# The hybrid decoder step: first tile's rows squared ahead of the second tile's, sampled rows' last scaling placed behind the copy of the compact scores

## Chip, cores, metric

One of the eight cores of a Trainium2 chip runs the whole program. The metric is the device time of one launch in microseconds (us).

## What is computed

One trunk layer for a prompt of 2048 tokens and for 64 sampled tokens (8 sequences of 8), all in float32:

```python
h = rms_norm(x, g_mix_pre)
proj = einsum('btd,de->bte', h, w_in)       # split: q, k, v | gq, gk, gv, gr, low-rank gate
attn = sliding window attention with sinks (8 heads of 64, 2 kv heads, window 128)
o, s_new = gla_chunked(gq, gk, gv, log_a, s0)          # 4 heads, dk 64, dv 128
gla_out = rms_norm(o, g_gla) * silu(gr)
mix = einsum('bte,ed->btd', concat([attn, gla_out]), w_out)
x = x + rms_norm(mix, g_mix_post)
h = rms_norm(x, g_ffn_pre)
u = relu(einsum('btd,df->btf', h, w_up))
f = einsum('btf,fd->btd', u * u, w_down)
x = x + rms_norm(f, g_ffn_post)
```

The outputs are the prompt's and the samples' rows, their last 128 keys and values, and the states of the gated linear attention (GLA).

## The kernel before

Rows lie in 17 tiles: 16 of 128 prompt rows (numbers 0 to 15) and one of the 64 sampled rows (number 16, `NB`). Each float32 product is made of three (high by high, high by low, low by high part), so an operand is first split: ScalarE (ACT) copies the high part, VectorE (DVE) subtracts it for the low part. TensorE (PE) is busy nearly all the time; the other engines prepare its operands and take its sums out of PSUM.

The program has these stages, one after the other: projection and attention (`unit`, `sample_unit`); GLA with the rest of the projection woven in (`gla`, `sampled`, `products`); the output projection with the residual rows (`out_projecting`, `residual`); the up projection (`up`, with `opening` as its first block); the down projection (`down`).

The code is written as generators that are advanced by `next` and `run`. Within what they write, a scheduler of the framework sets the order on each engine. `tc.issue_after(x)` ties an instruction behind another in that order and adds no semaphore between them. Each engine runs its instructions in order, so one that waits holds all behind it. DMAs are issued by SyncE (SP), also in order.

**GLA, one tile.** `gla` makes score products into the banks `gl` and `gh`, six masked copies on VectorE (`put_level`, COPY_PREDICATED) gather them into the compact scores `AH`, and VectorE (`put[0]`, line 1173) and ScalarE (lines 1172 and 1174) copy these into `AT`. Two VectorE instructions (line 1179) then bring the state `S` up to date. The products `o` read `AT`. `finish_out` ends a tile: squares, their mean to the power -0.5 on GpSimd (POOL; `rsqrt_mean`), and four scalings `og` on VectorE (line 1088), one for each head, whose transposes (`ogT`) follow. For the sampled rows the same function runs with `i == NB`: it reads the bank `s_ob`, writes the scaled rows into `gp_s`, and its transposes are put off by `S_WAIT[0]` further steps. It runs beside the GLA of a prompt tile.

**Output projection.** The tiles are taken in the order `B_ORDER` = 0, 4, 1, 5, 2, 6, 3, 7, 16, 8, 12, ... . A tile has 48 products (two halves of 512 columns, 8 parts of the sum, three each), into the banks `a` or `b` in turn. The first two tiles are multiplied at the end of the GLA stage. `mixed` then takes a tile's two banks: two squares (ScalarE, line 1412), their sum and the power -0.5, two scalings `x<-out` (VectorE, line 1419), and the add of the input row `bx` (line 1420). `residual` goes on: a square of the new row (`bjunk`, line 1510), the power, the scaling by `gpre` (line 1513), which gives the row that PE transposes (`xnT`, line 1523), and copies of the transposed row (`ht`, `H`).

The first tile (0) has its new rows early: `mixed_first` runs in the GLA stage and its result goes by a DMA (`mt<-x_first`, line 1422) into a place in the `mt` buffer of the third tile. What is left of it in the loop is the square of that place, the scaling and the transposes. The second tile (4) has all of `residual` left; it waits for its input rows (`bx<-in_x_prompt`). The `mt` buffers alternate, so the load of the fifth tile's operand (`mt<-mix_d`) waits until the third tile's products and the scaling that reads the first tile's rows are through.

Of the kernel before, what the change touches and what calls it, by code (L numbers as in the profile page):

```python
# [16 lines left out]
ALU = mybir.AluOpType  # L17
# [4 lines left out]
P = 128  # L22
# [3 lines left out]
NB = T // P  # L26
# [89 lines left out]
def f32(ap):  # L116
    return ap.bitcast(F32)
# [23 lines left out]
def hybrid_step_kernel(ctx: ExitStack, tc: tile.TileContext, I, O):  # L141
    nc = tc.nc
# [11 lines left out]
    def rows(i):  # L154
        return min(P, NTOK - i * P)
# [12 lines left out]
    def bank(shape, kind, name):  # L168

        return ps.tile(shape, F32, tag=kind, name=name, bufs=1 if kind in "de" else 2)  # L170
# [3 lines left out]
    def next_bank(kinds, name):  # L174
        turns[kinds] += 1
        return bank([P, 512], kinds[(turns[kinds] - 1) % len(kinds)], name)
# [26 lines left out]
    def rsqrt_mean(pool, out, ssq, n, m, c=1, vector=nc.vector):  # L203

        v = pool.tile([P, c], F32, tag="rs_v", name="rs_v", bufs=4)
        vector.tensor_scalar(v[:n], ssq, 1.0 / m, EPS, op0=ALU.mult, op1=ALU.add)  # L206
        e = half[:n] if c == 1 else half[:n].to_broadcast([n, c])
        nc.gpsimd.tensor_tensor(out, v[:n], e, op=ALU.pow)  # L208

    def folded(out, p_, scalar=nc.scalar, vector=nc.vector):  # L210

        scalar.activation(out, p_[NS:], AF.Copy)
        vector.tensor_tensor(out, out, p_[:NS], op=ALU.add)  # L213
        return out
# [68 lines left out]
    def load_x(i):  # L283
        xs_in[i] = x = sp.tile([P, D], F32, tag="x", name=f"x_{i}", bufs=2)
        nc.sync.dma_start(x[: rows(i)], x_rows(i))
        ropes[i] = sp.tile([P, 2, HD], F32, tag="rope", name=f"rope_{i}", bufs=4)
        nc.sync.dma_start(ropes[i], I["c_rope"][i])
# [386 lines left out]
    def run(products, n=None):  # L674
        deque(products if n is None else islice(products, n), 0)
# [95 lines left out]
    early, late = (deque((c, k) for c in cs for k in range(KT)) for cs in (G_EARLY, G_LATE))  # L771
# [303 lines left out]
    def finish_out(i, og_src, sg, n, kind):  # L1075

        ssq = sp.tile([P, 4], F32, tag="ossq", name=f"ossq_{i}", bufs=2)
        junk = sp.tile([P, P], mybir.dt.bfloat16, tag="ojunk", name=f"ojunk_{i}", bufs=1)
        for h in range(4):
            nc.scalar.activation(junk[:n], og_src(h), AF.Square, accum_out=ssq[:n, h : h + 1])  # L1080
        rs = sp.tile([P, 4], F32, tag="ors", name=f"ors_{i}", bufs=2)
        rsqrt_mean(sp, rs[:n], ssq[:n], n, P, 4)
        if i == NB:
            yield 44, True
            yield 44, True
        og = next(ogs) if i < NB else gp_s[:, :512].rearrange("p (h d) -> p h d", h=4)
        for h in range(4):
            nc.vector.scalar_tensor_tensor(
                og[:n, h, :], og_src(h), rs[:n, h : h + 1], sg[:n, h * P : (h + 1) * P],
                op0=ALU.mult, op1=ALU.mult,  # L1090
            )
        for _ in range(S_WAIT[0] if i == NB else 1):
            yield 44, True
        pt = bank([P, 4, P], kind, f"ogT_{i}")
        for h in range(4):
            te.transpose(pt[:, h, :n], og[:n, h, :], ident[:n, :n])
        if i == NB - 1:
            hi, lo = late_mix
            nc.vector.tensor_copy(hi, pt)
            nc.vector.tensor_tensor(lo, pt, f32(hi), op=ALU.subtract)  # L1100
        else:
            mo = next(mos)
            nc.scalar.activation(mo[:, :, :n], pt[:, :, :n], AF.Copy)
            nc.sync.dma_start(mix_d[i][:, 4:8, :], mo[:, :, :n])
# [303 lines left out]
    def mixed(i, banks, x, x1, junk, ssq, gpost, pool, scalar=nc.scalar, vector=nc.vector):  # L1408
        n = rows(i)
        for c in range(2):  # L1410
            cc = slice(c * 512, (c + 1) * 512)
            scalar.activation(junk[:n, cc], banks[c][:n], AF.Square, accum_out=ssq[:n, c : c + 1])
        vector.tensor_tensor(ssq[:n, 0:1], ssq[:n, 0:1], ssq[:n, 1:2], op=ALU.add)
        rs = ssq[:n, 3:4]
        rsqrt_mean(pool, rs, ssq[:n, 0:1], n, D, vector=vector)
        yield
        for c in range(2):
            cc = slice(c * 512, (c + 1) * 512)
            vector.scalar_tensor_tensor(x1[:n, cc], banks[c][:n], rs, gpost[c][:n], op0=ALU.mult, op1=ALU.mult)
        vector.tensor_tensor(x[:n], x1[:n], x[:n], op=ALU.add)  # L1420
        if x1_first and i == B_ORDER[0]:
            placing[:] = [nc.sync.dma_start(x1_first[0], x)]
        nc.sync.dma_start(x1_d[i], x[:n])

    wo, pre, ogs_of, mixes, late_mix, g_mix, put, placing, x1_first = {}, {}, {}, {}, [], [], [], [], []
    wo_parts = iter(())
    early = []
# [46 lines left out]
    def ht_place(name):  # L1474
        return keep.tile([P, 7, KT // 2, P], F32, tag="st", name=name, bufs=1)
# [21 lines left out]
    def residual(i, banks, tensor=nc.tensor, scalar=nc.scalar, vector=nc.vector):  # L1497

        n = rows(i)
        x = res_x.pop(i, None) or load_x(i)[0]  # L1500
        ssq = sp.tile([P, 48], F32, tag="ssq", name=f"bssq_{i}", bufs=2)
        junk = sp.tile([P, D], mybir.dt.bfloat16, tag="junk", name=f"bjunk_{i}", bufs=1)
        x1 = R["x"].tile([P, D], F32, tag="x1", name=f"x1_{i}", bufs=2)
        if i == NB:
            banks = [folded(x1[:NS, c * 512 : (c + 1) * 512], p_) for c, p_ in enumerate(banks)]
        if banks:
            g = g_mix if tensor is nc.tensor else [gpost[:, c * 512 : (c + 1) * 512] for c in range(2)]
            yield from mixed(i, banks, x, x1, junk, ssq, g, sp, scalar, vector)
        rs = ssq[:, 3:5]
        scalar.activation(junk[:n], x[:n], AF.Square, accum_out=ssq[:n, 2:3])  # L1510
        yield
        rsqrt_mean(sp, rs[:n, 1:2], ssq[:n, 2:3], n, D, vector=vector)
        vector.scalar_tensor_tensor(x1[:n], x[:n], rs[:n, 1:2], gpre[:n], op0=ALU.mult, op1=ALU.mult)
        yield
        sb, j, second = i // 8, i % 4, i % 8 >= 4
        q = slice(j * P, (j + 1) * P)
        if i < NB and not second and i:
            sums[sb, j] = ht_place(f"ht_{i}")
        for h in range(2):
            kk = slice(h * 4, h * 4 + 4)  # L1520
            pt = (bank([P, 512], "ce"[h], f"xnT_{i}_{h}") if te is tensor else next_bank("cdce", f"xnT_{i}_{h}")).rearrange("p (k t) -> p k t", k=4)
            for k in range(4):
                tensor.transpose(pt[:, k, :n], x1[:n, (h * 4 + k) * P : (h * 4 + k + 1) * P], ident[:n, :n])
            if i == NB:
                split_copy(xsT[:, kk, :NS], xsT[:, kk, NS:], pt[:, :, :NS], vector)
                continue
            ht = sums[sb, j]
            scalar.activation(ht[:, (6, 2)[h] if second else h], pt, AF.Copy)
            if sb == 0 and not second:
                split_copy(H[h + 1][0][:, :, q], H[h + 1][1][:, :, q], pt, vector)  # L1530
        if i == NB or not second:
            return
        yield
        for out, a, b in ((4, 6, 0), (6, 2, 6), (5, 2, 4), (3, 1, 5)):
            vector.tensor_tensor(ht[:, out], ht[:, a], ht[:, b], op=ALU.subtract)
        kept = slice(2 * (sb == 0), 7)
        nc.sync.dma_start(h_d[sb][:, kept, :, q], ht[:, kept])
# [55 lines left out]
    for n, i in enumerate(B_ORDER[2:]):  # L1593
        early.append((i, []))
        mixing = out_projecting(nc.tensor, i, early[-1][1])
        run(mixing, 24 if i == B_ORDER[-1] else 48)
        if n == 0:
            second = residual(*early.pop(1))
            next(second)
            next(second)  # L1600
        elif n == 1:
            run(second)
        if n != 1:
            run(residual(*early.pop(0)))
        run(mixing)
        if n == len(B_ORDER) - 5:
            with tc.issue_after(loaded.ins):
                first_up = load_up(0, 0)
            with tc.issue_after(first_up.ins):
                gpost = gains(I["g_mix_post"][0], 0, "gpost")  # L1610
            split_up(0, 0, 0)
            split_up(0, 0, 1)
            fetch_h(0, 5)
# [575 lines left out]
```

## Time and profile before

| | |
|---|---|
| time, median of 3 runs | 2207.52 us (2206.16 to 2207.61) |
| time of the profiled execution | 2206.11 us |
| its span | 2204.0 us |
| granted TensorE clock | 0.996 |
| busy: PE, DVE, ACT, POOL | 98%, 69%, 55%, 12% |

The span is what the instructions cover; 2.11 us of the execution's time lie outside it. In a timeline a row has a start, the time that a run of equal instructions covers, the engine, the line and the tiles (out<-in); in brackets stands how long the engine was idle before it and what released it.

### The profile page before, as it was taken

The page shows a single profiled execution, that of the slowest core. Times are in us where ns is not written, and L with a number is a line of the kernel's source. Part 1 is how long each engine was busy: PE and PEld are TensorE (multiplying, and loading weights), DVE is VectorE, ACT ScalarE, POOL GpSimd, SP SyncE. Part 2 cuts the span into 40 slices and gives each one's busy share as a digit, 9 for nine tenths or more (in the row PEclk, how much of TensorE's full clock was granted, in tenths as well). Part 3 has the DMA queues.
Part 4 walks back from the last instruction along what each step waited for, and adds up shares of the span by engine and source line. Part 5 has one row for each costly group of instructions (what it writes and reads, how often), then busy time and mean ns, then how long its engine had stood idle before and what let it go on. Part 6 is the DMA issues. An engine that isn't in the chain of part 4 may idle for free.

```text
span 2204.0 us, 34115 instructions
## 1 busy us (share of the span) xinstructions
PE 2163.2 (98%) x11784; PEld 1864.7 (85%) x11784; DVE 1531.4 (69%) x3101; ACT 1219.1 (55%) x2626; POOL 263.0 (12%) x418
## 2 busy tenths in 40 slices
PE   8999999999999999899999999999999999999998
PEld 7999989999998888688888887887888888888886
DVE  5888868777775665788888655547676666555566
ACT  5889867566664444555555544435444554444444
POOL 2566512121111100000000000000000000000000
PEclk9999999999999999999999999999999999999999
DMA  6344232214336665768777677758554334766685
GB/s 228 131 137 156 96 106 70 68 64 148 136 125 237 223 208 190 239 228 277 260 261 270 232 236 225 240 182 260 180 195 149 138 144 148 238 201 193 194 269 185
DMA packets 240185, 411.53 MB, mean 187 GB/s; under 512 B 25924, under 2 KB 142124, under 8 KB 235900
## 3 DMA queue, kind: packets, MB, share of 16 engines
q1 hardware_dynamic: 240012, 409.35, 55.9%
q8 instruction: 93, 1.52, 0.3%
q14 instruction: 80, 0.66, 0.1%
HBM read 265.82 MB, written 143.99 MB: 186 GB/s over the span
## 4 chain that ended last, share of the span: by engine, by line
PE 85%; DVE 6%; ACT 4%; DMA 2%; issue 1%; POOL 1%; SPq 0%; DVEq 0%; ACTq 0%; POOLq 0%
PE dn L130 26%; PE gproj L130 10%; PE uc L130 7%; PE ua L130 7%; PE out L1318 6%; PE proj L130 5%; PE ue L130 4%; PE ud L130 4%; PE ub L130 4%; PE av L130 1%; PE sam L130 1%; PE dsam L130 1%; PE o L130 1%; PE pT L130 1%; PE sc L130 1%
## 5 line engine op out<-in xcount | busy, mean ns | idle before, releaser
L130 PE MATMUL dn<-o0t,o0s 128*128 128x512 f32 x896 | 349.3, 390 | 2.8 <-DVE f L1891 1.5
L130 PE MATMUL dn<-o1t,o0s 128*128 128x512 f32 x896 | 349.5, 390 | 0.3 <-DVE o1t L219 0.2
L130 PE MATMUL dn<-o0t,o1s 128*128 128x512 f32 x896 | 349.4, 390 | 0.0
L219 DVE TENSOR_TENSOR o1s<-rs,o0s 128x512 fp32r<-128x512 f32 x224 | 154.7, 691 | 227.8 <-ACT o0s L218 223.7
L218 ACT ACTIVATE o0s<-rs 128x512 fp32r<-128x512 f32 x224 | 141.1, 631 | 305.5 <-PE dn L130 282.3
L130 PE MATMUL gproj<-wg,gxh 128*128 128x384 f32 x1024 | 272.5, 342 | 0.3 <-DVE gp_s L213 0.3
L130 ACT ACTIVATE st<-st 128x512 f32<-128x512 f32 x224 | 141.2, 630 | 140.7 <-DVE st L130 136.6
L130 PEld LDWEIGHTS dn<-o0t,o0s 128*128 128x128 f32 x896 | 168.3, 188 | 40.6 <-DVE f L1891 2.4
L130 PEld LDWEIGHTS dn<-o1t,o0s 128*128 128x128 f32 x896 | 168.2, 188 | 37.0 <-DVE o1t L219 1.1
L130 PEld LDWEIGHTS dn<-o0t,o1s 128*128 128x128 f32 x896 | 168.2, 188 | 35.0
L130 PEld LDWEIGHTS gproj<-wg,gxh 128*128 128x128 f32 x1024 | 183.8, 188 | 4.1 <-issue 3.1
L130 PE MATMUL uc<-H,s 128*128 128x512 f32 x768 | 186.8, 391 | 0.4 <-DVE s L130 0.4
L130 PE MATMUL gproj<-wg,gxl 128*128 128x384 f32 x576 | 186.0, 340 | 0.2 <-DVE gp_s L213 0.2
L130 PE MATMUL ua<-H,w 128*128 128x512 f32 x744 | 179.2, 390 | 0.0
L130 PEld LDWEIGHTS uc<-H,s 128*128 128x128 f32 x768 | 142.9, 188 | 31.2 <-DVE s L130 0.8
L130 PEld LDWEIGHTS ua<-H,w 128*128 128x128 f32 x744 | 139.7, 188 | 29.5
L1318 PE MATMUL out<-wo,mt 128*128 128x512 f32 x680 | 158.6, 392 | 0.0
L219 DVE TENSOR_TENSOR o1t<-rt,o0t 128x512 fp32r<-128x512 f32 x224 | 153.5, 685 | 7.0 <-ACT o0t L218 6.9
L208 POOL TENSOR_TENSOR frs<-rs_v,half 128x1 f32<-128x1 f32 (+1 forms) x13 | 10.1, 787 | 1214.4 <-DVE rs_v L206 694.5
L1318 PEld LDWEIGHTS out<-wo,mt 128*128 128x128 f32 x680 | 126.5, 188 | 26.1
L218 ACT ACTIVATE o0t<-rt 128x512 fp32r<-128x512 f32 x224 | 138.3, 618 | 8.9 <-DMA rt<-t_d 7.2
L130 DVE TENSOR_TENSOR st<-st 128x512 f32<-128x512 f32 x160 | 110.6, 692 | 27.0 <-ACT st L130 22.6
(405 smaller groups left out, 4322.3 us busy)
## 6 DMA issues: line engine op xcount, KB each, us to landing
s_d<-st SPq DMA_DIRECT2D x32, 1792.0 KB, 8.7
rs<-s_d SPq DMA_DIRECT2D x224, 256.0 KB, 2.8
raw<-in_w_up SPq DMA_DIRECT2D x64, 512.0 KB, 4.3
rt<-t_d SPq DMA_DIRECT2D x128, 256.0 KB, 4.1
rt<-in_w_down SPq DMA_DIRECT2D x96, 256.0 KB, 3.1
t<-in_w_down SPq DMA_DIRECT2D x64, 256.0 KB, 4.0
t_d<-t SPq DMA_DIRECT2D x32, 512.0 KB, 3.2
hraw<-h_d SPq DMA_DIRECT2D x20, 512.0 KB, 5.1
```

The lines of the kernel that those rows point to most:

```text
L130: ins = call(*a, **k)
L208: nc.gpsimd.tensor_tensor(out, v[:n], e, op=ALU.pow)
L218: nc.scalar.activation(hi, src, AF.Copy)
L219: vector.tensor_tensor(lo, src, f32(hi), op=ALU.subtract)
L1318: te.matmul(banks[c], x, w[:, c * 512 : (c + 1) * 512], start=k + u == 0, stop=k == KT - 1 and u == len(products) - 1,)
```

## The change

Two edits. In `finish_out`, the four scalings of the sampled rows are tied behind `put[0]`, the VectorE copy of the compact scores of the prompt tile that runs beside them. In the loop of the output projection, the first tile's generator is advanced to its square before the second tile's is begun, and run to its end after the second tile's square.

```diff
@@ finish_out
         for h in range(4):
-            nc.vector.scalar_tensor_tensor(
-                og[:n, h, :], og_src(h), rs[:n, h : h + 1], sg[:n, h * P : (h + 1) * P],
-                op0=ALU.mult, op1=ALU.mult,
-            )
+            with tc.issue_after(put[0].ins) if i == NB else nullcontext():
+                nc.vector.scalar_tensor_tensor(
+                    og[:n, h, :], og_src(h), rs[:n, h : h + 1], sg[:n, h * P : (h + 1) * P],
+                    op0=ALU.mult, op1=ALU.mult,
+                )
@@ the loop over B_ORDER[2:]
         if n == 0:
-            second = residual(*early.pop(1))
+            first_rows = residual(*early.pop(0))
+            next(first_rows)
+            second = residual(*early.pop(0))
             next(second)
             next(second)
+            run(first_rows)
         elif n == 1:
             run(second)
-        if n != 1:
+        else:
             run(residual(*early.pop(0)))
```

What this does to the order on the engines, at three places. First VectorE in the GLA stage, where the sampled rows end (`gp_s` their scaled rows, `AH` the compact scores, `AT` and `S` as above). Before:

```order
L206 TENSOR_SCALAR rs_v<-ossq_6665 64x4
L1088 SCALAR_TENSOR_TENSOR gp_s<-s_ob,ors_6671,s_sg 64x128
L1063 COPY_PREDICATED AH<-c_1573,gl_6679 128x128
L1088 SCALAR_TENSOR_TENSOR gp_s<-s_ob,ors_6671,s_sg 64x128
L1063 COPY_PREDICATED AH<-c_1573,gl_6679 128x64x2
L1088 SCALAR_TENSOR_TENSOR gp_s<-s_ob,ors_6671,s_sg 64x128
L1063 COPY_PREDICATED AH<-c_1573,gl_6679 128x32x4
L1088 SCALAR_TENSOR_TENSOR gp_s<-s_ob,ors_6671,s_sg 64x128
L1063 COPY_PREDICATED AH<-c_1573,gl_6679 128x16x8
L1063 COPY_PREDICATED AH<-c_1573,gh_6680 128x8x16
L1063 COPY_PREDICATED AH<-c_1573,gh_6680 128x4x32
L1173 COPY AT<-AH 64x4x64
```

The same place after the change:

```order
L206 TENSOR_SCALAR rs_v<-ossq_6665 64x4
L1063 COPY_PREDICATED AH<-c_1573,gl_6679 128x128
L1063 COPY_PREDICATED AH<-c_1573,gl_6679 128x64x2
L1063 COPY_PREDICATED AH<-c_1573,gl_6679 128x32x4
L1063 COPY_PREDICATED AH<-c_1573,gl_6679 128x16x8
L1063 COPY_PREDICATED AH<-c_1573,gh_6680 128x8x16
L1063 COPY_PREDICATED AH<-c_1573,gh_6680 128x4x32
L1174 COPY AT<-AH 64x4x64
L1180 SCALAR_TENSOR_TENSOR S_4967<-S_4968,dec_4983,ds_6707 128x128 x2
L1089 SCALAR_TENSOR_TENSOR gp_s<-s_ob,ors_6671,s_sg 64x128 x4
L1073 COPY_PREDICATED AH<-dmsk,dg_6831 128x256
```

The four scalings leave their places between the copies and stand behind the update of the state.

Second, ScalarE at the start of the loop (`out_0_9241` and `out_1_9465` are the second tile's banks, `bx_9554` its rows, `mt_9446` holds the first tile's rows, `xnT_0_9628` its transposed rows, `out_0_9556` is a bank of the third tile, `raw_0_0` a block of `w_up`). Before:

```order
L218 ACTIVATE mt_9548<-mt_9548 128x1024
L1412 ACTIVATE bjunk_9607,bssq_9606<-out_0_9241 128x512
L1412 ACTIVATE bjunk_9607,bssq_9606<-out_1_9465 128x512
L1510 ACTIVATE bjunk_9607,bssq_9606<-bx_9554 128x1024
L1510 ACTIVATE bjunk_9621,bssq_9620<-mt_9446 128x1024
L1580 ACTIVATE w_0_0_10699<-raw_0_0_10693 128x1024
L1412 ACTIVATE bjunk_9772,bssq_9771<-out_0_9556 128x512
L1412 ACTIVATE bjunk_9772,bssq_9771<-out_1_9581 128x512
L1528 ACTIVATE ht_9547<-xnT_0_9628 128x512
```

After:

```order
L218 ACTIVATE mt_9548<-mt_9548 128x1024
L1511 ACTIVATE bjunk_9607,bssq_9606<-mt_9446 128x1024
L1413 ACTIVATE bjunk_9611,bssq_9610<-out_0_9241 128x512
L1413 ACTIVATE bjunk_9611,bssq_9610<-out_1_9465 128x512
L1529 ACTIVATE ht_9547<-xnT_0_9628 128x512
L1511 ACTIVATE bjunk_9611,bssq_9610<-bx_9554 128x1024
L218 ACTIVATE H_0_9515<-xnT_0_9628 128x4x128
L1529 ACTIVATE ht_9547<-xnT_1_9636 128x512
L218 ACTIVATE H_0_9517<-xnT_1_9636 128x4x128
L1413 ACTIVATE bjunk_9772,bssq_9771<-out_0_9556 128x512
L218 ACTIVATE mt_9715<-mt_9715 128x1024
L1413 ACTIVATE bjunk_9772,bssq_9771<-out_1_9581 128x512
```

The square of the first tile's rows goes ahead of the second tile's squares, the two high parts of `w_up` fall behind the third tile's squares, and the split of the fifth tile's operand (`mt_9715`) now stands between those squares. On VectorE the scaling of the first tile's rows (line 1513, now 1514) goes ahead of the add of the second tile's input rows. On SP the second block of `w_up` and the fifth tile's operand go ahead of the store of the second tile's rows (`x_d<-bx`).

Third, TensorE in the fourth tile's products (`out_0_9644`), at the first tile's transposes. Before, they stand behind 17 of the fourth tile's products:

```order
L1318 MATMUL out_0_9644<-wo_2_9177,mt_9548 128x512 x2
L1318 MATMUL out_0_9644<-wo_2_9178,mt_9548 128x512
L1523 MATMUL xnT_0_9628<-ident,x_0_9622 128x128 x4
L1523 MATMUL xnT_1_9636<-ident,x_0_9622 128x128 x4
L1318 MATMUL out_0_9644<-wo_2_9177,mt_9548 128x512
```

After, behind the first four:

```order
L1319 MATMUL out_0_9644<-wo_1_9058,mt_9548 128x512
L1319 MATMUL out_0_9644<-wo_1_9059,mt_9548 128x512
L1319 MATMUL out_0_9644<-wo_1_9058,mt_9548 128x512 x2
L1524 MATMUL xnT_0_9628<-ident,x_0_9608 128x128 x4
L1524 MATMUL xnT_1_9636<-ident,x_0_9608 128x128 x4
```

The transposes stand 13 products earlier.

## The prediction

> **What bounds the kernel now.** I read the page first, then what TensorE waits for, then the timeline of each engine around its waits. The page:
>
> ```profile
> span 2204.0 us, 34115 instructions
> PE 2163.2 (98%) x11784; PEld 1864.7 (85%) x11784; DVE 1531.4 (69%) x3101; ACT 1219.1 (55%) x2626; POOL 263.0 (12%) x418
> ```
>
> TensorE is busy for 2163.2 of 2204.0 us, and the change takes no product away. It can only gain from the 40.8 us in which TensorE stands, and only where TensorE itself waits. Three rows of the waits of TensorE (what waits, for whom, us in total, times, longest):
>
> ```profile
> PE ua L130 <- ACT s L130: 3.0, 1, 3.0
> PE xnT L1523 <- DVE x L1513: 1.6, 1, 1.6
> PE o L130 <- DVE S L1179: 1.4, 2, 0.7
> ```
>
> The second and one of the two waits of the third belong to the places that the change touches. The first comes later, in the opening of the up projection, and matters for whether a gain is kept.
>
> **The first tile's rows.** The timeline of TensorE at the start of the loop:
>
> ```profile
> 709.50 15.02 PE L1318 MATMUL out<-wo,mt 128*128 128x512 f32 x65
> 726.10 1.06 PE L1523 MATMUL xnT<-ident,x 128*128 128x128 f32 x8 [1.58 <-DVE x L1513]
> 726.92 7.34 PE L1318 MATMUL out<-wo,mt 128*128 128x512 f32 x31
> 734.89 7.32 PE L1318 MATMUL out<-wo,mt 128*128 128x512 f32 x31
> ```
>
> 65 products (48 of the third tile, 17 of the fourth) end at 724.52, and the transposes wait 1.58 us for the scaled rows. A product takes 15.02 / 65 = 0.231 us. Why the rows are late is seen on ScalarE and VectorE:
>
> ```profile
> 712.76 1.06 ACT L218 ACTIVATE mt<-mt 128x1024 fp32r<-128x1024 f32 x1 [7.17 <-DMA mt<-mix_d]
> 713.72 0.58 ACT L1412 ACTIVATE bjunk<-out 128x512 bf16<-128x512 f32 x1
> 721.50 1.06 ACT L1510 ACTIVATE bjunk<-bx 128x1024 bf16<-128x1024 f32 x1 [6.53 <-DVE bx L1420]
> 722.68 1.06 ACT L1510 ACTIVATE bjunk<-mt 128x1024 bf16<-128x1024 f32 x1
> ```
> ```profile
> 715.00 0.16 DVE L1413 TENSOR_TENSOR bssq<-bssq 128x1 f32<-128x1 f32 x1
> 716.08 1.41 DVE L1419 SCALAR_TENSOR_TENSOR x<-out,bssq,wo 128x512 f32<-128x512 f32 x2 [0.72 <-POOL bssq L208]
> 720.17 1.23 DVE L1420 TENSOR_TENSOR bx<-x,bx 128x1024 f32<-128x1024 f32 x1 [2.69 <-DMA bx<-in_x_prompt]
> 724.67 1.28 DVE L1513 SCALAR_TENSOR_TENSOR x<-mt,bssq,gpre 128x1024 f32<-128x1024 f32 x1 [0.59 <-POOL bssq L208]
> ```
>
> The first tile's square (of `mt`, 722.68) stands behind the second tile's (of `bx`, 721.50), for which ScalarE idles 6.53 us: the second tile's add waits for its input rows, which land at 720.08 (the chain's row below). The first tile's rows need none of that.
>
> With the change the first tile's square starts at A, when the copy of `mt` is done (712.76 + 1.06 = 713.82) and its own rows have landed. From there: 1.18 to the next ScalarE instruction (722.68 - 721.50), 1.28 for the second tile's two squares (715.00 - 713.72), 1.08 to its scalings (716.08 - 715.00), 1.41 for these, 1.28 for the first tile's scaling, 0.15 to the transposes (726.10 - 725.95). Together 6.38 us. The power of the first tile runs on GpSimd meanwhile. The landing of the first tile's rows is not in a row by itself; its neighbours in SP's queue are:
>
> ```profile
> 711.27 0.50 SPq L1422 DMA_DIRECT2D mt<-x_first  x1
> 712.46 0.78 SPq L1479 DMA_DIRECT2D gpre<-in_g_ffn_pre  x1
> 715.08 0.69 SPq L1576 DMA_DIRECT2D raw<-in_w_up  x1
> 721.81 0.43 SPq L1576 DMA_DIRECT2D raw<-in_w_up  x1
> 726.10 0.33 SPq L1278 DMA_DIRECT2D mt<-mix_d  x1
> ```
> ```profile
> mt<-mix_d SPq DMA_DIRECT2D x3, 512.0 KB, 3.8
> x_d<-bx SPq DMA_DIRECT2D x3, 512.0 KB, 2.6
> x_d<-x_first SPq DMA_DIRECT2D x1, 512.0 KB, 4.2
> ```
> ```profile
> 713.28 6.80 DMA bx<-in_x_prompt
> ```
>
> Transfers of the same 512 KB take 2.6 us from issue to landing alone and 4.2 in company, so the rows issued at 711.27 land between 713.9 and 715.5; I take 714.7, midway, since the one ahead in the queue is already under way. The transposes are then ready at 714.7 + 6.38 = 721.1 (bounds 720.3 to 721.9). The gain `gpre` must be there by 719.7; it is issued between `mt<-x_first` and `bx`, and `bx` has landed by 713.28 + 6.80 = 720.08, so at the very worst the rows are 0.4 us later, 721.5. TensorE reaches the transposes 13 products earlier than before, at 724.52 - 13 x 0.231 = 721.5. So the wait of 1.58 us goes, with 0.4 us to spare by my values and up to 0.4 us of wait left at the late bound of the landing. **Term 1: -1.58 us, bounds -1.2 and -1.58.**
>
> What else moves there. The second tile's banks come free at 714.7 + 1.18 + 1.28 + 1.08 + 0.7 (half of 1.41) = 718.9 and 719.7 instead of 716.8 and 717.5; the fourth tile's first product needs the first of them at 709.50 + 48 x 0.231 = 720.6, so 1.7 us of cover remain. The second tile's add would start at 720.9 in place of 720.17, and its square stands behind the first copy of the transposed rows and so starts about 722.6, 1.1 us later than 721.50; its own transposes come only after the 31 products that end at 726.92 + 7.34 = 734.26, so this is covered by several us. The second `w_up` block is issued some 6 us earlier (right behind 715.08 instead of 721.81), behind `bx` in the queue; nothing on TensorE needs it in this stage. The fifth tile's operand is issued when the third tile's products and the first tile's scaling are through, about 721, not 726.10, and lands near 721 + 3.8 = 724.8. That matters since the third tile's second square now waits behind its split on ScalarE: 1.06 + 0.64 + 1.08 for split, square and power, two VectorE instructions of 1.23 and half a pair of scalings, 0.7, make 5.9, so the third tile's first bank is free near 730.7. The fifth tile needs it at 734.89 less what is gained, 732.6: 1.9 us of cover.
>
> **The sampled rows.** The rows of TensorE, VectorE and ScalarE there:
>
> ```profile
> 475.09 0.86 PE L130 MATMUL gh<-XQ,XK 128*64 128x64 f32 x20
> 481.01 0.49 PE L130 MATMUL o<-gp,AT 128*128 128x128 f32 x2 [0.74 <-DVE S L1179]
> 493.60 0.46 PE L130 MATMUL ogT<-ident,gp_s 64*128 64x64 f32 x4
> ```
> ```profile
> 476.04 0.16 DVE L206 TENSOR_SCALAR rs_v<-ossq 64x4 f32<-64x4 f32 x1 [1.89 <-ACT ojunk L1080]
> 477.32 0.34 DVE L1088 SCALAR_TENSOR_TENSOR gp_s<-s_ob,ors,s_sg 64x128 f32<-64x128 f32 x1 [1.12 <-POOL ors L208]
> 477.59 0.43 DVE L1063 COPY_PREDICATED AH<-c,gl 128x128 f32<-128x128 uint8 x1
> 480.36 0.61 DVE L1179 SCALAR_TENSOR_TENSOR S<-S,dec,ds 128x128 f32<-128x128 f32 x2
> 480.99 0.45 DVE L1073 COPY_PREDICATED AH<-dmsk,dg 128x256 f32<-128x256 uint8 x1
> ```
> ```profile
> 480.56 0.40 ACT L1174 ACTIVATE AT<-AH 64x256 f32<-64x256 f32 x1
> ```
>
> VectorE waits 1.12 us for GpSimd's power with the six copies of the compact scores behind it, though what the copies read was finished at 475.95. The copies start at 477.59, `AT` is whole at 480.96 on ScalarE, and TensorE waits 0.74 us for it. How long the copies take with nothing between them is seen one tile later:
>
> ```profile
> 498.50 1.59 DVE L1063 COPY_PREDICATED AH<-c,gl 128x128 f32<-128x128 uint8 x4
> 501.38 0.41 ACT L1174 ACTIVATE AT<-AH 64x256 f32<-64x256 f32 x1
> ```
>
> From the first copy to `AT` are 501.79 - 498.50 = 3.29 us there, against 480.96 - 477.59 = 3.37 here: the three scalings between them cost 0.08 in all, and what is gained is the start. With the change the copies follow `rs_v`, at about 476.25, and `AT` is whole at 479.54. TensorE wants it at 481.01 - 0.74 = 480.27, so the wait goes with 0.7 us to spare (0.6 if the copies took 3.37 as now). Behind the state (480.97 - 1.4 = 479.55) the four scalings then take about 4 x 0.3 = 1.2 us, so the next copy starts at 480.75, still ahead of 480.99; their transposes come at 493.60, 12.8 us later. **Term 2: -0.74 us, the same at both ends.**
>
> **The sum.** -1.58 - 0.74 = -2.32 us. The profiled execution took 2206.11 (2.11 outside its span), 1.41 under the median of the runs and 0.05 under the lowest. On its scale I expect 2203.8; on that of the median, 2207.52 - 2.32 = **2205.2**. That is 0.1%, under the 0.2% (4.4 us) which a measurement of this kernel can tell from no change.
>
> **Rivals.** *A, late in part.* The first tile's rows are ready after TensorE arrives and 0.2 to 1.5 us of the wait stay. For: my spare is 0.4 us on an inferred landing. Against: `mt<-x_first` has only one transfer ahead of it. Time 2205.4 to 2206.7, say 2206.0.
>
> *B, given back later.* TensorE arrives 2.32 us sooner at the opening of the up projection, where it waits for ScalarE and VectorE anyway:
>
> ```profile
> 884.83 1.03 PE L1523 MATMUL xnT<-ident,x 128*128 128x128 f32 x8
> 903.37 0.73 PE L130 MATMUL ua<-H,s 128*128 128x512 f32 x2 [2.97 <-ACT s L130]
> ```
>
> If what ends that wait does not come sooner, the gain turns into a longer wait: 2207.5. Against it: that work (the last tiles' rows, stored, fetched again and split) starts from the last sums and transposes of TensorE before 885.9, so it should move with them.
>
> *C, slower.* The transposes now stand 3.0 us earlier in TensorE's row of products, and so do all products behind them. If what the first tile's scaling needs (its rows, or `gpre`) lands late, TensorE meets the wait early. Point: with term 2 counted, the kernel is slower from a wait of 2.32, scaled rows ready after 723.8, which is a landing of `mt<-x_first` after 717.4 or of `gpre` after 722.4 (1.28 + 0.15 ahead of the transposes). If `mt<-x_first` landed with `bx` at 720.08, its rows would be ready at 726.46, the wait be 4.96, and the time 2207.5 + 4.96 - 2.32 = 2210.2. Against: `x_d<-x_first`, issued behind it, has landed 4.2 us after 711.82, at 716.0, and `bx`, issued behind `gpre`, at 720.08; only the second `w_up` block is new beside them, and it stands behind them in the queue. The Trainium skill bears on this rival (DMA: Bandwidth & Descriptors, "Latency and other measured facts"): access to HBM costs 0.2 us on average and up to 2 us at high load, so that a fuller queue could delay `gpre` by up to 1.8 us. The trace agrees in kind, with 2.6 us for a transfer alone and 4.2 in company. By that figure, as an estimate, `gpre` would land at 721.9 at the latest, the rows be ready at 723.3 and the wait be 1.8: a time of 2207.0.
>
> *D, more than counted.* With loads issued sooner, the opening's waits shrink too: of the 2.97 us some 1 to 2.5, giving 2202.7 to 2204.2. For it I see only that two loads are issued 5 to 6 us earlier, 160 us ahead of that place.
>
> **How the numbers follow.** The forecast (both waits gone and kept) has 0.62, A 0.15, B 0.13, C 0.06, D 0.04. The range: from 2203.4 (the lowest run, 2206.16, less 2.32, and a little of D) to 2207.8 (B with the highest run, 2207.61); C's far end and D's are left out. D's best end comes to 4.8 us below the median, over the 4.4: 0.03 of its 0.04. C reaches 4.4 us above it only with a landing beyond 721.8: half of its 0.06, 0.03. Within 0.2%: 0.94.
>
> **What would show it.** Right: no wait of `xnT` on the scaled rows among TensorE's waits, and its transposes starting near 720.8 (721.5 less 0.74) in place of 726.10; the wait of `o` for `S` or `AT` down to one of 0.6; the square of `mt` ahead of the squares of `out`; the opening's 2.97 unchanged. Wrong: a wait of `xnT` over 0.5 us (A or C), a longer wait of `ua` or `ud` (B), or a new wait of `out` for a bank, which I count as covered by 1.7 and 1.9 us.

## The result, and the profile after

The changed kernel takes 2204.1 us (median of 18 runs, 2201.76 to 2207.04), the kernel before 2206.97 on the same chips (18 runs, 2204.75 to 2209.49). The ratio is 0.9985, with a 95% interval of 0.9978 to 0.9992: 2.87 us less, with the whole interval below 1 (1.8 to 4.9 us less); the ratio lies inside the 0.2% that the prediction counted as no change. The profiled execution took 2204.05 us, its span is 2202.3 us. From its page:

```profile
PE 2163.6 (98%) x11784; PEld 1865.5 (85%) x11784; DVE 1532.1 (70%) x3101; ACT 1219.5 (55%) x2626; POOL 263.5 (12%) x418
```

No engine does less. What changed is TensorE's list of waits (what waits, for whom, us in total, times, longest). The wait of `xnT` for the scaled rows is gone, of the two waits of `o` one is left, `ua` is as it was, and below it the waits of the opening are dealt out anew (`sam` was 2.0, `ud` 1.8). Four rows:

```profile
PE ua L130 <- ACT s L130: 3.0, 1, 3.0
PE sam L130 <- ACT both L130: 1.4, 2, 0.8
PE ud L130 <- ACT H L130: 1.1, 1, 1.1
PE o L130 <- DVE S L1180: 0.6, 1, 0.6
```

The first tile's rows. TensorE's timeline after the change; no bracket stands behind any row, so nothing waits:

```profile
709.32 12.08 PE L1319 MATMUL out<-wo,mt 128*128 128x512 f32 x52
721.24 1.03 PE L1524 MATMUL xnT<-ident,x 128*128 128x128 f32 x8
722.03 10.27 PE L1319 MATMUL out<-wo,mt 128*128 128x512 f32 x44
732.93 2.33 PE L1319 MATMUL out<-wo,mt 128*128 128x512 f32 x9
```

ScalarE, VectorE and GpSimd there, one fence each. ScalarE waits 0.44 us for the first tile's rows and squares them; VectorE scales the second tile, then (718.97) the first. The last rows of each fence belong to the fifth tile's operand (726.89) and the third tile's power and scalings:

```profile
714.09 1.06 ACT L1511 ACTIVATE bjunk<-mt 128x1024 bf16<-128x1024 f32 x1 [0.44 <-DMA mt<-x_first]
726.89 1.06 ACT L218 ACTIVATE mt<-mt 128x1024 fp32r<-128x1024 f32 x1 [1.35 <-DMA mt<-mix_d]
```
```profile
717.64 1.41 DVE L1420 SCALAR_TENSOR_TENSOR x<-out,bssq,wo 128x512 f32<-128x512 f32 x2 [0.66 <-POOL bssq L208]
718.97 1.27 DVE L1514 SCALAR_TENSOR_TENSOR x<-mt,bssq,gpre 128x1024 f32<-128x1024 f32 x1
731.17 1.41 DVE L1420 SCALAR_TENSOR_TENSOR x<-out,bssq,wo 128x512 f32<-128x512 f32 x2 [0.43 <-POOL bssq L208]
```
```profile
723.77 0.54 POOL L208 TENSOR_TENSOR bssq<-rs_v,half 128x1 f32<-128x1 f32 x1 [5.66 <-DVE rs_v L206]
729.64 1.49 POOL L208 TENSOR_TENSOR bssq<-rs_v,half 128x1 f32<-128x1 f32 x1 [5.33 <-ACT w L1581]
```

The scaled rows are ready at 718.97 + 1.27 = 720.24, a microsecond before TensorE comes for them.

The sampled rows, on VectorE, ScalarE and TensorE. The copies start right behind `rs_v`, the four scalings behind `S`:

```profile
476.86 0.16 DVE L206 TENSOR_SCALAR rs_v<-ossq 64x4 f32<-64x4 f32 x1 [1.88 <-ACT ojunk L1080]
476.93 1.57 DVE L1063 COPY_PREDICATED AH<-c,gl 128x128 f32<-128x128 uint8 x4
480.12 1.11 DVE L1089 SCALAR_TENSOR_TENSOR gp_s<-s_ob,ors,s_sg 64x128 f32<-64x128 f32 x4
```
```profile
479.79 0.40 ACT L1175 ACTIVATE AT<-AH 64x256 f32<-64x256 f32 x1
```
```profile
480.71 0.38 PE L130 MATMUL o<-S,qd 128*128 128x128 f32 x2
480.93 0.39 PE L130 MATMUL o<-gp,AT 128*128 128x128 f32 x2
```

**Where the 2.87 us come off.** Runs of one kernel spread over 5 us, so a difference of two executions says little by itself; cut into stages it says more. Four rows of TensorE's timeline bound the stages: the first product of the GLA stage, of the output projection, the last tile's transposes, and the first product of the down projection. Before, then after:

```profile
280.02 0.34 PE L130 MATMUL gproj<-wg,gxh 128*128 128x384 f32 x1
682.32 2.02 PE L130 MATMUL out<-wo,mt 128*128 128x512 f32 x8
898.63 1.03 PE L130 MATMUL xnT<-ident,x 128*128 128x128 f32 x8
1241.38 0.39 PE L130 MATMUL dn<-o0t,o0s 128*128 128x512 f32 x1
```
```profile
280.58 0.34 PE L130 MATMUL gproj<-wg,gxh 128*128 128x384 f32 x1
682.14 2.02 PE L130 MATMUL out<-wo,mt 128*128 128x512 f32 x8
896.64 1.03 PE L130 MATMUL xnT<-ident,x 128*128 128x128 f32 x8
1239.80 0.39 PE L130 MATMUL dn<-o0t,o0s 128*128 128x512 f32 x1
```

The differences of neighbouring starts, with the same four rows read in each experiment's trace (us; the last column is the median time less that of the kernel before in the same comparison; the down projection, which is left out, takes 961.2 to 963.6):

| kernel | to GLA | GLA | output projection | opening and up | median |
|---|---|---|---|---|---|
| before | 280.02 | 402.30 | 216.31 | 342.75 | |
| changed | 280.58 | 401.56 | 214.50 | 343.16 | -2.87 |
| 1: scalings only | 280.00 | 401.29 | 216.39 | 343.02 | -0.48 |
| 2: rows only | 282.29 | 402.28 | 214.49 | 342.90 | -2.54 |
| 3: rows land second | 281.85 | 401.28 | 215.20 | 342.91 | -1.67 |
| 4: rows land late | 282.04 | 401.26 | 222.09 | 343.21 | +2.78 |
| 5: power twice, before | 278.60 | 403.30 | 216.59 | 343.40 | +1.01 |
| 6: transposes behind the tile | 278.88 | 401.32 | 214.88 | 343.42 | -2.93 |
| 7: power twice, changed | 279.42 | 401.29 | 214.52 | 343.03 | -2.59 |
| 8: sums ahead | 278.89 | 401.25 | 214.50 | 344.69 | -2.08 |

The GLA stage falls into three groups that follow one edit: 402.3 without the tie, 401.3 to 401.6 with it, 403.3 with the doubled power and no tie. The output projection follows the other edit: 216.3 to 216.6 without it, 214.5 with it (experiments 3, 4 and 6 change more there). The first stage, which no kernel touches, wanders over 3.7 us. A cut close to the edit is sharper still. From the products `o` at the sampled rows to the end of the GLA stage the two kernels take 202.43 us before (682.32 - 479.89) and 201.43 after (682.14 - 480.71); experiment 2, without the tie, takes 202.44, experiment 5 203.45, and the six others with the tie in place 201.42 to 201.45. So the tie is worth 1.00 us, and the 0.27 us by which the changed kernel's GLA stage is longer than experiment 1's lie ahead of the place that it touches.

### The profile page after: what moved, and what is told of

It reads as the page before. It is cut to its first block, busy times and chain, and to the rows that moved or that the text cites. A ratio compares the mean times of both kernels' runs of the same rounds, so it can differ in the third digit from the quotient of the medians.

```text
span 2202.3 us, 34117 instructions
## 1 busy us (share of the span) xinstructions
PE 2163.6 (98%) x11784; PEld 1865.5 (85%) x11784; DVE 1532.1 (70%) x3101; ACT 1219.5 (55%) x2626; POOL 263.5 (12%) x418
## 4 chain that ended last, share of the span: by engine, by line
PE 86%; DVE 5%; ACT 4%; DMA 2%; issue 1%; POOL 1%; SPq 0%; DVEq 0%; ACTq 0%; POOLq 0%
PE dn L130 26%; PE gproj L130 11%; PE uc L130 7%; PE ua L130 7%; PE out L1319 7%; PE proj L130 5%; PE ud L130 4%; PE ue L130 4%; PE ub L130 4%; PE sam L130 1%; PE dsam L130 1%; PE av L130 1%; PE o L130 1%; PE out L130 1%; PE pT L130 1%
```

## Experiments

### 1 and 2: each edit alone

Experiment 1 keeps the tie and has the loop as before:

```diff
-            first_rows = residual(*early.pop(0))
-            next(first_rows)
-            second = residual(*early.pop(0))
+            second = residual(*early.pop(1))
             next(second)
             next(second)
-            run(first_rows)
         elif n == 1:
             run(second)
-        else:
+        if n != 1:
             run(residual(*early.pop(0)))
```

> Only the tie of the sampled rows' scalings behind the copy of the compact scores; the first tile's rows stay as before. My theory (two separate waits of TensorE, which add): the wait of the products o for AT and S at this place (0.74 us before) goes, the wait of xnT for the scaled rows stays at 1.6 us; time 0.74 us under the kernel before. Rival (the gain was all in the order of the first tile's rows, and the scalings only move work on VectorE): no change of the time, since the copies start no earlier or TensorE waits at the next place instead.

Measured: 2206.57 us against 2207.05, ratio 0.9994 (0.9986 to 1.0003). On TensorE's timeline the products run through at the sampled rows, and the transposes wait as before:

```profile
480.08 0.39 PE L130 MATMUL o<-gp,AT 128*128 128x128 f32 x2
```
```profile
725.21 1.06 PE L1524 MATMUL xnT<-ident,x 128*128 128x128 f32 x8 [1.72 <-DVE x L1514]
```

Experiment 2 takes the tie out and keeps the order of the rows (the call's arguments, left out here, move one step to the left):

```diff
-            with tc.issue_after(put[0].ins) if i == NB else nullcontext():
-                nc.vector.scalar_tensor_tensor(
+            nc.vector.scalar_tensor_tensor(
```

> Only the new order of the first tile's rows; the sampled rows' scalings stay between the copies. My theory: the wait of xnT goes, the wait of o of 0.74 us stays; time 1.6 us under the kernel before. Rival (given back later): the wait in the opening of the up projection, 2.97 us, grows by what is gained, and the time is that of before.

Measured: 2204.51 us, ratio 0.9987 (0.9978 to 0.9996). The one wait is back, the other is not:

```profile
483.26 0.49 PE L130 MATMUL o<-gp,AT 128*128 128x128 f32 x2 [0.75 <-DVE S L1179]
```
```profile
723.67 1.03 PE L1523 MATMUL xnT<-ident,x 128*128 128x128 f32 x8
```

In the stages the two edits don't touch each other: each moves its own and leaves the other as it was. Experiment 1 alone can't be told from no change by its time (its interval holds 1), but its stage can: 401.29 in place of 402.30. That the time of experiment 2 fell by 2.54 where its stage fell by 1.82 lies within its interval, 0.9 to 4.9 us.

### 3 and 4: landing the first tile's rows later

These measure the rival that the changed order becomes slower when the rows land late. Experiment 3 issues the store of the first tile's rows ahead of the copy into `mt`:

```diff
-            placing[:] = [nc.sync.dma_start(x1_first[0], x)]
-        nc.sync.dma_start(x1_d[i], x[:n])
+            stored = nc.sync.dma_start(x1_d[i], x[:n])
+            with tc.issue_after(stored.ins):
+                placing[:] = [nc.sync.dma_start(x1_first[0], x)]
+        else:
+            nc.sync.dma_start(x1_d[i], x[:n])
```

> The changed kernel with two DMAs swapped: the store of the first tile's rows to DRAM goes ahead of the transfer that puts them where they are squared. My theory: that transfer lands when the store does now, near 715.8 instead of 714.0, the square starts at 715.85, the scaled rows are ready 6.3 us later at 722.15, and TensorE, which arrives at 721.25, waits 0.9 us; time 0.9 us over the changed kernel. Rival (there is more cover than I counted, since the second tile's work may fill the gap): no wait.

Measured: 2205.38 us, ratio 0.9990 (0.9981 to 0.9999). The square waits 1.93 us in place of 0.44, and a third of the 1.49 us more reaches TensorE:

```profile
716.58 1.06 ACT L1514 ACTIVATE bjunk<-mt 128x1024 bf16<-128x1024 f32 x1 [1.93 <-DMA mt<-x_first]
```
```profile
722.89 1.06 PE L1527 MATMUL xnT<-ident,x 128*128 128x128 f32 x8 [0.51 <-DVE x L1517]
```

So 1.93 - 0.44 - 0.51 = 0.98 us is what the changed kernel has to spare there; the wait is 0.51 us where 0.9 was expected. The time alone can't show so small a step. The stage is 215.20 - 214.50 = 0.70 longer for a wait of 0.51; the section on the prediction shows why.

Experiment 4 stores the rows to memory and reads them back into `mt` behind the second tile's input rows, so that they land near 722; the scheduler puts the transposes 5 products further back:

```diff
-            placing[:] = [nc.sync.dma_start(x1_first[0], x)]
-        nc.sync.dma_start(x1_d[i], x[:n])
+            placing[:] = [nc.sync.dma_start(x1_d[i], x[:n])]
+        else:
+            nc.sync.dma_start(x1_d[i], x[:n])
@@ behind the load of the second tile's input rows
+    with tc.issue_after(loaded.ins):
+        nc.sync.dma_start(x1_first[0], x1_d[B_ORDER[0]])
```

> The changed kernel, but the first tile's rows are read back from DRAM behind the second tile's input rows instead of coming by the early transfer. The scheduler puts the transposes five products later. My theory (rival C of the prediction as a mechanism): the rows land near 721.4, are scaled 6.3 us later at 727.8, and TensorE, whose arrival is 722.4, loses 5.4 us in all, split between the fourth tile's first product, which waits for the second tile's bank near 725.7, and the transposes; time 5.4 us over the changed kernel and 2.9 over the one before. Rival (the order on TensorE gives way, or other engines' work moves into the gap): under 2 us over the changed kernel.

Measured: 2209.83 us, ratio 1.0016 (1.0007 to 1.0024): slower than the kernel before. ScalarE and TensorE:

```profile
721.91 1.06 ACT L1514 ACTIVATE bjunk<-mt 128x1024 bf16<-128x1024 f32 x1 [7.02 <-DMA mt<-x_d]
```
```profile
726.36 4.18 PE L1319 MATMUL out<-wo,mt 128*128 128x512 f32 x9 [4.71 <-DVE x L1420]
730.34 1.81 PE L1527 MATMUL xnT<-ident,x 128*128 128x128 f32 x8
```

The prediction's rival C is real as a mechanism, and its place is another than the prediction gave; the expectation ahead of this run had the bank already. The square of `mt` stands at the head of ScalarE's queue, so it holds the second tile's squares; these hold its scalings, and the fourth tile's first product waits for the bank, before any transposes are reached. The products behind the wait take 4.18 / 9 = 0.46 us each, not 0.23. The window that begins at 726 (us, busy time and count of each engine: PE, PEld, DVE, ACT, POOL; then the granted clock, DMA share, GB/s):

```profile
726.00:732.00 6.00, 5.64 (x18) 4.70 (x19) 5.47 (x6) 1.63 (x3) 0.00 (x0) 0.51 0.47 164
```

At a clock of 0.51 for 6 us TensorE loses about 2.9 us more (an estimate: 6 x 0.49). With it the 7.59 us by which this execution's stage is over the changed kernel's are accounted for, with a wait of 4.71. The runs of this kernel reach from 2208.03 to 2215.58 us; the six under 2210 have a mean clock of 0.995 or 0.996, the five over 2211 one of 0.992 to 0.994.

### 5 and 7: a later norm for the sampled rows

Both experiments take the power of the sampled rows' norms on GpSimd twice, which makes the norms one power later; experiment 5 adds it to the kernel before, experiment 7 to the changed one:

```diff
         rsqrt_mean(sp, rs[:n], ssq[:n], n, P, 4)
         if i == NB:
+            rsqrt_mean(sp, rs[:n], ssq[:n], n, P, 4)
             yield 44, True
```

> The kernel before with one thing added: at the sampled rows GpSimd takes the power that gives the norms twice, one behind the other. Theory (the norms end last for the three free scalings of the kernel before only as long as VectorE has them queued ahead of the score copies): the copies start later by one power, some 0.5 to 1.0 us, the wait of the products for the copied scores grows from 0.74 to about 1.3 to 1.8, and the time rises by the same, to about 2207.6 to 2208.1 with the kernel before at 2207.05. Rival (the wait is set by something else than VectorE's order): the wait stays at 0.74 and the time within noise of the kernel before.

> The changed kernel with the power of the sampled rows taken twice. Theory: the norms are needed only by scalings that now stand behind the copy of the scores, so the later norms (0.5 to 1.0 us) are covered: no wait at the products over the copied scores, the wait of 0.6 us at the products over S within 0.2 of itself, time as the changed kernel within 0.3 us. Rival (the scalings were near to ending last): a wait of up to 1 us at the products that read the scaled rows, and the time up by as much.

Measured: experiment 5 2207.85 us against 2206.84, ratio 1.0004 (0.9996 to 1.0013); experiment 7 2204.25, ratio 0.9988 (0.9979 to 0.9996). VectorE and TensorE in experiment 5, where the copies wait with the first scaling:

```profile
476.96 0.34 DVE L1089 SCALAR_TENSOR_TENSOR gp_s<-s_ob,ors,s_sg 64x128 f32<-64x128 f32 x1 [2.13 <-POOL ors L208]
```
```profile
480.58 0.49 PE L130 MATMUL o<-gp,AT 128*128 128x128 f32 x2 [1.74 <-ACT AT L1175]
```

And in experiment 7, where they don't, though the two powers are as long (2.08 us in both traces):

```profile
475.57 1.57 DVE L1063 COPY_PREDICATED AH<-c,gl 128x128 f32<-128x128 uint8 x4
```
```profile
479.49 0.39 PE L130 MATMUL o<-gp,AT 128*128 128x128 f32 x2
```

VectorE's wait grows by 1.01 us (1.12 to 2.13), TensorE's by 1.00 (0.74 to 1.74) and the stage by 1.00: before the change the power of the sampled rows was passed on to TensorE whole, through VectorE's order alone. With the tie the same microsecond costs nothing: the stage is 401.29 us, and the wait of `o` for `S` stays at 0.6. Here too the times alone can't tell (experiment 5's interval holds 1); the stages do.

### 6: where the transposes stand

The changed kernel with the first tile's transposes behind all of the fourth tile's products instead of 52 products into the loop; the square stays early:

```diff
             next(second)
             next(second)
+        elif n == 1:
             run(first_rows)
-        elif n == 1:
             run(second)
```

> The changed kernel, but the rest of the first tile's rows (its transposes too) stands behind the whole fourth tile's products instead of 52 into it; its square stays in front of the second tile's. Theory (the gain is the earlier square; where the transposes stand is free as long as the scaled rows are there): no wait at either tile's transposes, time as the changed kernel, about 2204.1 to 2204.5. Rival (the transposes' place pays by itself): the scalings on VectorE now stand behind the second tile's residual, a wait of 0.5 to 1.7 us at the transposes comes back and the time is 0.5 to 1.7 us over the changed kernel.

Measured: 2203.91 us, ratio 0.9987 (0.9978 to 0.9995), the same as the changed kernel. TensorE has no wait there:

```profile
707.38 22.05 PE L1319 MATMUL out<-wo,mt 128*128 128x512 f32 x96
729.27 1.91 PE L1524 MATMUL xnT<-ident,x 128*128 128x128 f32 x16
731.31 3.89 PE L1319 MATMUL out<-wo,mt 128*128 128x512 f32 x16
```

So that the transposes stand 13 products earlier pays nothing by itself. The run doesn't show that the square had to be earlier, though: with the transposes behind 96 products, the kernel before would come for the rows near 709.50 + 96 x 0.229 = 731.5, and it had them ready at 725.95. Moving only the transposes back should remove the wait as well; that was not run. What ties the changed kernel's gain to the earlier square is that, with the transposes at their early place, its wait comes back when the rows land later (experiment 3).

The stage is 0.38 us longer than the changed kernel's, and VectorE shows why:

```profile
730.42 0.75 DVE L1420 SCALAR_TENSOR_TENSOR x<-out,bssq,wo 128x512 f32<-128x512 f32 x1 [1.03 <-PE xnT L1524]
```

The fifth tile's first product starts 0.14 us after this scaling of the third tile, which frees its bank, is done (730.42 + 0.75 = 731.17, then 731.31). The cover of that bank is used up here, in a wait that is too short for a bracket.

### 8: the largest wait that is left

The changed kernel with the sums behind the 2.97 us wait of `ua`, and their split, put ahead of the split of the hidden activations:

```diff
         elif p == 2:
             taken(p)
             next(last_rows)
+            sums_24(0, 0, dv)
+            split_sums(0, 0, 24, ac, dv)
             run(load_h(0, 6, ac, dv))
@@ p == 8
-            sums_24(0, 0, dv)
-            split_sums(0, 0, 24, ac, dv)
```

> The changed kernel with one step of the up projection's opening put earlier: the 24 sums of the first tile's up projection and their split stand ahead of the split of the first six tiles of the hidden activations on VectorE and ScalarE, instead of behind it. It is aimed at the largest wait that is left there, 2.97 us of TensorE for the split sums. Theory (that wait is set by the order on ScalarE and VectorE): it falls to 0.6 us or less and the time by up to 2.4 us, to about 2201.7. Rival (the split of the hidden activations becomes what ends last): the later waits of the opening (1.07 and 0.76) grow by what the first one loses, and the time stays within 0.5 us of the changed kernel.

Measured: 2204.76 us, ratio 0.9990 (0.9981 to 0.9999); nothing gained over the changed kernel, and its opening is 1.53 us longer. TensorE's largest wait in the opening, and ScalarE's row:

```profile
PE uc L130 <- ACT H L130: 3.1, 1, 3.1
```
```profile
902.82 1.06 ACT L130 ACTIVATE H<-H 128x1024 fp32r<-128x1024 f32 x1 [3.83 <-DMA H<-h_d]
```

The wait of `ua` is gone, `sam` waits 1.90 us in place of 0.59, and the next products wait 3.13 us for `H`: the activations that come back from memory end last. That is the rival, at the fetch rather than at the splits that the text named.

## Why the prediction was right

**Term 1, the first tile's rows: right, sized a little low.** The wait went. The landing taken midway, 714.7, was 714.09 at the latest by the start of the square, inside its bounds; from there to the transposes 6.38 us were counted, and 720.24 + 0.15 - 714.09 = 6.30 ran. TensorE came at 721.24, so 0.85 us by the rows and 0.98 by experiment 3 were spare, where 0.4 had been worked out. One reading was off: the 2.6 us that the landing's early bound rests on are the median of three stores, and the one issued at 721.43 was not alone, since a block of `w_up` was issued behind it at 721.81.

**Term 2, the sampled rows: right in the same way.** From the first copy to `AT` 3.29 us were counted and 480.19 - 476.93 = 3.26 ran; the copies started 0.07 behind `rs_v`, not 0.21. `AT` was whole 0.74 ahead of its product (0.7 predicted), and the scalings took 1.11 us (1.2). Experiments 5 and 7 show the mechanism.

**The sum: the step that was mis-sized is that a wait was taken for its idle time.** -2.32 was predicted; the stages show -1.00 at the sampled rows and -1.81 (216.31 to 214.50) at the first tile's, together -2.81. The median fell by 2.87, but its interval holds 2.32 as well as 2.81, so only the stages show the difference. An idle time runs from the end of the product ahead, but in a stream the next product starts before that end. Without a wait the products at `AT` follow those at `S` after 480.93 - 480.71 = 0.22 us, though these are shown as 0.38 long; with the wait, before, they started at 481.01 after a row that began at 479.89:

```profile
479.89 0.38 PE L130 MATMUL o<-S,qd 128*128 128x128 f32 x2
481.34 0.39 PE L130 MATMUL o<-S,qd 128*128 128x128 f32 x2
```

That is 1.12 us in place of 0.22: the wait of 0.74 cost 0.90. The products behind it were slower too: the next ones follow after 481.34 - 481.01 = 0.33 us, after the change after 0.22. With these 0.11 the cost is 1.01, all that the stage shows. Likewise at the transposes. The last product ahead of them, before and after:

```profile
724.14 0.39 PE L1318 MATMUL out<-wo,mt 128*128 128x512 f32 x1
```
```profile
721.01 0.39 PE L1319 MATMUL out<-wo,mt 128*128 128x512 f32 x1
```

The transposes start 726.10 - 724.14 = 1.96 us behind it before the change and 721.24 - 721.01 = 0.23 after: the wait of 1.58 cost 1.73. Each wait costs about 0.16 us more than its bracket, the part of the last product that overlaps the next in a stream; experiment 3's 0.70 for a wait of 0.51 fits too. The profile's ends of products are modelled, so the 0.16 belongs to the bracket; the 0.90 and 1.73 come from starts alone. The Trainium skill (TensorE: Matmul & The Clock Gate, "Single matmul latency" and "Step-by-step: what each phase is for") says that a product's drain overlaps the next product, with a constant of about 0.17 us for drain and issue that only an isolated product shows (it gives it for bf16). The rows agree: 0.38 - 0.22 = 0.16.

**The covers: one right, one mis-sized, none broken.** The fourth tile's bank: free at 717.64 + 0.70 = 718.34, wanted at 709.32 + 48 x 0.229 = 720.3, so 2.0 us (1.7 predicted). The fifth tile's: 732.93 less 731.87, 1.06 us (1.9 predicted). Its operand was issued at 720.56, as predicted near 721, but was there for ScalarE only at 726.89, 6.3 us later instead of 3.8; the power behind it took 1.49 us on GpSimd in place of 0.54. The 1.35 us that ScalarE waits there were paid from the cover. That so much of the cover was left is in part luck: with the load 2.1 and the power 0.95 us later than counted, the bank was free only 1.2 later (731.87, not 730.7), because one of the two VectorE instructions that were counted in the path ran beside the power (`w`, at 729.51). The median of three landings did not price a load that is issued at another place; what it shares the DMA engines with there was not taken apart.

**Rivals.** *A* (part of the wait stays) fell: no wait of `xnT`. *B* (given back in the opening) and *D* (more gained there) both fell (`ua` waits 2.97 us in both kernels), and here a list of waits misleads. The idle times of TensorE over 0.25 us between 885 and 945, added up from the trace, fell from 8.4 to 7.9 us, which looks like half a microsecond of D; but the stage took 342.75 before and 343.16 after. TensorE ran at a lower clock in these executions (before, then after):

```profile
885.00:945.00 60.00, 51.59 (x228) 40.72 (x227) 44.65 (x57) 31.94 (x51) 1.95 (x2) 0.94 0.71 230
```
```profile
885.00:945.00 60.00, 52.09 (x223) 40.96 (x222) 43.57 (x57) 30.63 (x48) 1.95 (x2) 0.91 0.68 223
```

Apart from experiment 8 all kernels take 342.75 to 343.42 there, with no order that follows an edit. *C* (slower) did not happen, but experiment 4 makes it happen: 2209.83 us measured, where the prediction priced a landing with `bx` at 2210.2. Its place was wrong, the bank of the second tile and not the transposes, and over a third of the 7.59 us in its profiled execution was the clock.

What stays open: the output projection shows 0.08 us more than the 1.73 of its wait, of which the slower transposes behind it make up 0.03 (0.82 us to the next product, not 0.79). Whether moving the transposes alone would do as well is open too.

## What to carry to other kernels

An instruction that nobody needs soon, queued on an in-order engine ahead of one that TensorE needs, hands its own wait on in full; tie it behind, and its lateness is free up to its own reader. Look for the engine that idles for one operand while the operand of the instruction behind it has landed. Where a change is smaller than the spread of the runs, cut two traces at the same instructions and compare stages: here a stage of 400 us gave the edit's worth to about 0.3 us, a cut that starts right ahead of the edit to 0.03, and the spread sat in the other stages. A wait on TensorE that is cut away in one place is worth its idle time and about 0.16 us of overlap, and, where the clock fell behind it as in experiment 4, that too; a wait that only moves to the next operand, as in experiment 8, is worth nothing.

## What the chip showed that was not expected

Part of the spread between executions of one kernel is TensorE's clock. The longer runs of the kernel before have the lower mean clock (correlation -0.69 over 33 runs in one comparison, -0.60 over 35 in another). Within a trace the granted clock is either whole or half, and a half-speed spell there lasts 3.41 us or twice that (the first 20 us and the last 15 left out). One and the same wait brings a spell in one execution and none in the next. In the first stage the products `av` wait 1.82 us in the kernel before and 1.80 in the changed one. The windows there, before, then after:

```profile
109.50:112.92 3.42, 1.25 (x8) 0.91 (x8) 1.20 (x5) 2.62 (x8) 3.34 (x5) 1.00 0.13 28
112.92:116.33 3.41, 3.41 (x16) 3.41 (x15) 2.30 (x8) 1.92 (x5) 1.32 (x3) 0.50 0.88 283
```
```profile
109.55:112.96 3.41, 1.96 (x12) 1.62 (x10) 1.59 (x6) 1.24 (x3) 3.12 (x6) 1.00 0.01 1
112.96:116.38 3.42, 2.73 (x20) 2.53 (x21) 2.59 (x8) 2.77 (x9) 2.45 (x4) 1.00 0.49 112
```

The windows are pieces of a grid of 3.41 us on which all spells of a trace begin and end. In the kernel before, the wait (109.65 to 111.47) lies in one piece, TensorE is busy for 1.25 of its 3.42 us, and the next piece runs at 0.50. In the changed kernel the wait (111.51 to 113.31) lies across two pieces, TensorE is busy for 1.96 and 2.73 us, and no spell follows. Counted over the ten traces, 34 spells begin from the whole clock. Ahead of 32 of them TensorE was busy for at most 0.52 of the piece; for the other two (0.57 and 0.64, both in the first 60 us) the cause stays open. Of all pieces at the whole clock that no spell follows, none was busy for less than 0.49. So what counts in these traces is not the length of a wait but whether it leaves a piece of the grid less than about half busy, and that changes with the start of the kernel on the grid. A piece at half the clock costs up to 1.7 us (an estimate: 3.41 x 0.5), and the first stage shows it: it takes 278.6 to 280.0 us in the five traces with at most one piece at half the clock, and 280.02 to 282.3 in the five with two or three.

The Trainium skill (TensorE: Matmul & The Clock Gate, "What's actually happening") describes a clock that is halved by a monitor with a free-running window of about 3.4 us, so that its phase differs from run to run. The traces agree with the half rate, the window and the change of place, but here a window that was about half busy, with waits of 1 to 2 us in it, was enough.
